# Gated attention outputs turned by transposing transfers, and one joining copy moved on ScalarE, in a two-layer encoder trunk

## Chip, cores and metric

The kernel runs on one core of a Trainium2 chip. The metric is the device time of one execution in microseconds (us), the median of several runs.

## The reference

The program is two layers of a hybrid encoder block over 256 tokens (two halves of 128, called `hf` 0 and 1 below) with a model width of 1024. Cut to the parts that matter here:

```
u = rms_norm(h, g_mix_pre)
(gq, gk, gv, gg, ra_f, ra_b, aq, ak, av, gate_a, gate_b) = split(u @ w_in)
o_gla    = rms_norm(o_f + o_b, g_gla_out)             # gated linear attention, both directions
branch_a = (o_gla * silu(gg)) @ w_o_gla               # 256x1024 @ 1024x1024
branch_b = gqa_attention(q, k, v) @ w_o_attn
mixed    = sigmoid(gate_a) * branch_a + sigmoid(gate_b) * branch_b
h = h + rms_norm(mixed @ w_out, g_mix_post)
gate, up = split(rms_norm(h, g_ffn_pre) @ w_ffn_in)   # 2 x 2816 columns
h = h + rms_norm((silu(gate) * up) @ w_ffn_out, g_ffn_post)
h = h + rms_norm(sigmoid(h @ w_ple_gate) * (p[i] @ w_ple_proj), g_ple_post)
```

The change concerns `o_gla * silu(gg)`, which has to stand feature by token before it can be the stationary operand of the product with `w_o_gla`, and `silu(gate) * up`, which has to be turned in the same way for `w_ffn_out`.

## The kernel before

All matrix products run on TensorE with each fp32 operand split into a high and a low fp32r part (`split`, L132: ScalarE casts the high part, VectorE subtracts it from the source for the low part), in three passes (`passes`, L122, and `mm`, L106). Weights are streamed from HBM in units of 128x2048 words (1 MB). `Stream` (L247) holds two raw buffers and four pairs `wh`/`wl`; a unit is one load on SP's queue, two 128x1024 casts on ScalarE and two 128x1024 subtractions on VectorE (all L134). A unit's raw buffer is loaded again once VectorE has subtracted from it. TensorE needs 24 matmuls of 128x512 for a plain unit (two token halves), and 12 for a unit inside a group of seven products that replace eight (`seven`, L713; weights in tiles `lent` and `big`, with 128x2048 additions on VectorE, L326 to L337).

Work that is not a weight product is written as `Task`s (L376): generators that are stepped by `tick` (L398), twice per twelve large matmuls or so, and that say after how many ticks they go on. So a number such as `W["g"]` or `WAIT_TURNED` sets where in the instruction order a step is put. Each engine executes its own instructions in that order; `tc.high_priority` and `tc.issue_after` move single ones.

Two ways of turning a block of 128 tokens x 512 features stand in the code:

- `transpose_in` (L445): four TensorE transposes against an identity matrix (L449) into a PSUM bank, then `split` from there.
- `turn_out` and `take_in` (L455, L472), used for the FFN's hidden values: ScalarE takes the 32-bit words apart into two planes of 16 bits (L468, or L463 where a block holds both token halves), SP issues one transposing transfer SBUF to SBUF (L469) of 128 x 1024 16-bit values, and `WAIT_TURNED` = 9 ticks later ScalarE joins the planes again (the "joining copy", L476), after which `split` works from SBUF.

The gate stage. `out_gate` (L1451) computes `sg = sigmoid(gg) * gg * o_gla` for each token half (L1457 on ScalarE, four 128x512 multiplications on VectorE, L127) and calls `turn_in` (L549), which waits 6 ticks and runs `transpose_in` on both 512-column blocks into `gT`. `GATES` = "uuu1u2m34m5m67m" (L1536) sets the order around it: u are the units of gate A, digits the seven products of gate B, m the four units of `gT @ w_o_gla`; `out_gate` must be done before the first m. TensorE's names there are `acc_0gate` (layer 0) and `acc_1gate`.

The FFN. The first two blocks of 256 hidden columns are computed by token half; after each half, the 512 values of both blocks (`first`) go to `turned` (L1573), which calls `turn_out` and, 9 ticks later, `take_in`. Each call takes a new 128x1024 tile `mid` for planes and result. The other blocks go the same way; only the last pair is turned by `transpose_in`.

SP's queue issues all weight loads and all transposing transfers in order: an entry that waits for its operand holds up those behind it.

Of the kernel before, what the change touches and what calls it, by code (L numbers as in the profile page):

```python
# [13 lines left out]
U16 = mybir.dt.uint16  # L14
# [4 lines left out]
P = 128  # L19
T = 256  # L20
# [9 lines left out]
WAIT_NEXT, WAIT_IN, WAIT_H = (7, 9), ((6, 9), (6, 6)), ((3, 5), (3, 5))  # L30
WAIT_MIX = 3, 6
WAIT_SPREAD = 12
W = dict(r=5, z=6, s0=4, s=3, s1=9, o0=1, o=1, k=4, q=3, a0=1, a1=4, a2=4, a3=1, g=6)

STEPS_FIRST = "00 10 01 11 02 12 03 13".split()
STEPS = "00 01 02 10 03 11 12 13".split()
# [24 lines left out]
def trunk_kernel(ctx: ExitStack, tc: tile.TileContext, a: dict, out: bass.AP):  # L61
# [7 lines left out]
    nc = tc.nc  # L69
# [11 lines left out]
    part = ["start"]  # L81
# [8 lines left out]
    def mid(dt=F32):  # L90
        return b4p.tile([P, 1024], dt, tag="mid", name=nm("mid"))
# [40 lines left out]
    def split(hi, lo, src):  # L132

        return nc.scalar.copy(hi, src), nc.vector.tensor_tensor(out=lo, in0=src, in1=hi.bitcast(F32), op=ALU.subtract)  # L134


    h = cp.tile([P, 2, D], F32, tag="h", name="h")
# [314 lines left out]
        if plain is not None:  # L452
            nc.scalar.copy(plain, ps[:, : n * P])

    def turn_out(src, k, hf):  # L455

        with tc.high_priority(AHEAD):
            both, turned = halves(mid())
            turned = turned.bitcast(U16)
            parts = both.bitcast(U16).rearrange("p (s c) -> p s c", s=2)  # L460
            words = src.bitcast(U16)
            if hf is None:
                nc.scalar.copy(  # L463
                    parts.rearrange("p s (k h f) -> p s k h f", k=2, f=P),
                    words.rearrange("p (h k f s) -> p s k h f", h=2, f=P, s=2),
                )
            else:
                nc.scalar.copy(parts, words.rearrange("p (c s) -> p s c", s=2))  # L468
            nc.sync.dma_start_transpose(out=turned.rearrange("p (x t) -> p x t", t=P), in_=parts.rearrange("p s c -> p (s c)"))  # L469
        return both, turned  # L470

    def take_in(sp, both, turned, k, hf):  # L472

        n, tn = (2, T) if hf is None else (4, P)
        hi, lo = sp.at(k, n, (hf or 0) * P, tn)
        nc.scalar.copy(  # L476
            both.bitcast(U16).rearrange("p (k t s) -> p k t s", s=2, t=tn),
            turned.rearrange("p (s k t) -> p k t s", s=2, t=tn),
        )
        split(hi, lo, both.rearrange("p (k t) -> p k t", t=tn))  # L480

    last_pow = [None]

# [62 lines left out]
    def halves(t):  # L546
        return [t[:, j * 512 : (j + 1) * 512] for j in range(2)]

    def turn_in(sp, x, hf, wait, plain=None, apart=False):  # L549


        def turn():
            yield wait
            for j, y in enumerate(halves(x)):
                if j and apart:
                    yield 1
                transpose_in(sp, y, 4 * j, 4, hf, plain and plain[j])

        sp.makers[hf].append(Task(turn(), part[0]))
# [489 lines left out]
    for l in range(DEPTH):  # L1049
# [31 lines left out]
        def put_ranks(o, hf):  # L1081
# [9 lines left out]
            with tc.high_priority(EMPTY):  # L1091
# [7 lines left out]
                nc.vector.tensor_copy(r[:, :, 64:80], r[:, :, 0:16])  # L1099
            yield W["r"]  # L1100
            ps = aux()
# [57 lines left out]
        o = {}  # L1159
# [20 lines left out]
        def keys(o):  # L1180
# [19 lines left out]
            for hf in range(2):  # L1200
                yield W["k"]
                ps = aux()
# [57 lines left out]
        def attend(g):  # L1260
            qs = []
            for hf in range(2):
                yield W["q"]
                ps = aux()
# [6 lines left out]
            keys.need()  # L1271
            yield W["a0"]
            prs = []
            for hf in range(2):
                prs.append(softmax(g, hf, qs[hf]))
                yield W["a1"]
            for hf in range(2):
# [21 lines left out]
        for x in range(2):  # L1299
            for i, o in enumerate(project_t(uT)):  # L1300
                dst, r = qk[:, x, i, :], 1.0 if x else P**-0.5
# [141 lines left out]
        gg = big().rearrange("p (s c) -> p s c", s=2)  # L1443
        for j in range(2):
            o = project(uT)
            for hf in range(2):
                dst = gg[:, hf, j * 512 : (j + 1) * 512]
                nc.scalar.activation(dst, o[hf], AF.Copy, bias=0.0, scale=rows[hf])
        gT = Split()

        def out_gate():  # L1451
            while not (gla.over and attention.over):
                yield 1
            for hf in range(2):
                sg = mid()
                with tc.issue_after(last_exp[0].ins):
                    nc.scalar.activation(sg, gg[:, hf, :], AF.Sigmoid)  # L1457
                for j, t in enumerate(halves(sg)):
                    s = slice(j * 512, (j + 1) * 512)
                    vmul(t, t, gg[:, hf, s])  # L1460
                    vmul(t, t, on[:, hf, s])
                turn_in(gT, sg, hf, W["g"])

        ogate = Task(out_gate(), f"{l}gg")

# [101 lines left out]


        part[0] = f"{l}ffnin"
        hid = Split()  # L1570
        us = [[ws.take() for _ in range(2)] for _ in range(2)]

        def turned(src, k, hf):  # L1573

            def turn():
                if k == 2 * PAIRS[-1]:
                    yield WAIT_LAST[hf]
                    transpose_in(hid, src, k, 4, hf)
                else:
                    x = turn_out(src, k, hf)  # L1580
                    yield WAIT_TURNED
                    take_in(hid, *x, k, hf)

            t = Task(turn(), part[0], k // 4)
            for i in range(2) if hf is None else (hf,):
                hid.makers[i].append(t)

        for hf in range(2):
            ws.lend = hf == 1
            first = t512()  # L1590
            for b in range(2):
                o = acc()
                for kh in range(2):
                    amode(o, u2, hf, kh * 4, us[b][kh], kh == 0, kh == 1, fresh=b == 0)
                sg = first[:, b * 256 : (b + 1) * 256]
# [35 lines left out]
        o = []  # L1631
# [21 lines left out]
        for x in FFN:  # L1653
# [3 lines left out]
            if x == "o":  # L1657
                n, w = outs.pop(0), ws.take()
# [117 lines left out]
```

## Time and profile before

| | us |
|---|---|
| median of 3 runs | 910.03 (909.97 to 911.33) |
| the profiled execution | 909.68 |
| its span (first to last instruction) | 907.9 |
| TensorE busy / VectorE busy / ScalarE busy | 898.8 / 790.2 / 620.5 |
| gate stage with merge, layer 0 / layer 1 (TensorE on `acc_gate`, then `acc_merge`) | 135.4 to 223.9 / 591.3 to 679.8 |

The profiled execution lies 0.35 us under the median, and 1.78 us of it are outside its span. In the rows of the profile, a start is given in us from the span's beginning, followed by the duration; `x4` is the count of like instructions merged into the row; a bracket such as `[0.55 <-DMA lent_0gate]` is the time for which the engine was idle before the row, and what ended that.

### The profile page before, as it was taken

The page shows a single profiled execution, that of the slowest core. Times are in us where ns is not written, and L with a number is a line of the kernel's source. Part 1 is how long each engine was busy: PE and PEld are TensorE (multiplying, and loading weights), DVE is VectorE, ACT ScalarE, POOL GpSimd, SP SyncE. Part 2 cuts the span into 40 slices and gives each one's busy share as a digit, 9 for nine tenths or more (in the row PEclk, how much of TensorE's full clock was granted, in tenths as well). Part 3 has the DMA queues.
Part 4 walks back from the last instruction along what each step waited for, and adds up shares of the span by engine and source line. Part 5 has one row for each costly group of instructions (what it writes and reads, how often), then busy time and mean ns, then how long its engine had stood idle before and what let it go on. Part 6 is the DMA issues. An engine that isn't in the chain of part 4 may idle for free.

```text
span 907.9 us, 12157 instructions
## 1 busy us (share of the span) xinstructions
PE 898.8 (99%) x4479; PEld 762.2 (84%) x4479; DVE 790.2 (87%) x1021; ACT 620.5 (68%) x1011; POOL 105.9 (12%) x157
## 2 busy tenths in 40 slices
PE   9999999999999999999999999999999999999997
PEld 8898888888888887887898888888888888888886
DVE  7999989987668999998779899799876799999984
ACT  7688677564467787756676687675644796958563
POOL 3700221300100000000254001110000000000001
PEclk9999999999999999999999999999999999999999
DMA  8663445657397594956576424455573966858461
GB/s 283 219 189 136 140 140 191 216 187 249 115 288 204 173 301 146 317 170 233 180 279 204 168 93 140 139 186 185 186 241 100 309 180 206 254 210 264 150 231 47
DMA packets 108519, 178.16 MB, mean 196 GB/s; under 512 B 22494, under 2 KB 46566, under 8 KB 107948
## 3 DMA queue, kind: packets, MB, share of 16 engines
q1 hardware_dynamic: 108300, 177.25, 59.9%
q8 instruction: 35, 0.57, 0.3%
q14 instruction: 24, 0.20, 0.1%
q10 hardware_dynamic: 160, 0.14, 0.0%
HBM read 169.50 MB, written 3.15 MB: 190 GB/s over the span
## 4 chain that ended last, share of the span: by engine, by line
PE 78%; DVE 11%; DMA 4%; issue 4%; ACT 2%; POOL 0%; SPq 0%; POOLq 0%; ACTq 0%; DVEq 0%
PE acc_1ffnin L122 12%; PE acc_0gate L122 7%; PE acc_1gate L122 7%; PE acc_1ffnin L106 7%; DVE wl_0ffnin L134 6%; PE acc_1rq L122 3%; PE acc_0gqk L106 2%; PE acc_1gqk L106 2%; PE acc_1wout L122 2%; PE acc_0ple L122 2%; PE acc_1v L122 2%; PE acc_0gg L122 2%; PE acc_1gg L122 2%; PE acc_0v L122 2%; PE acc_0merge L122 2%
## 5 line engine op out<-in xcount | busy, mean ns | idle before, releaser
L134 ACT CAST wh_0ffnin<-raw_0ffnin 128x1024 fp32r<-128x1024 f32 x38 | 38.1, 1048 | 19.8 <-DMA raw_0ffnin<-in_w_ffn_out_dram 10.2
L134 ACT CAST wh_1ffnin<-raw_1ffnin 128x1024 fp32r<-128x1024 f32 x38 | 38.3, 1048 | 17.4 <-DMA raw_1ffnin<-in_w_ffn_out_dram 5.0
L134 DVE TENSOR_TENSOR wl_0ffnin<-raw_0ffnin,wh_0ffnin 128x1024 fp32r<-128x1024 f32 x38 | 44.6, 1219 | 5.8 <-ACT wh_0ffnin L134 5.8
L134 DVE TENSOR_TENSOR wl_1ffnin<-raw_1ffnin,wh_1ffnin 128x1024 fp32r<-128x1024 f32 x38 | 44.8, 1219 | 5.0 <-ACT wh_1ffnin L134 4.9
L106 PE MATMUL acc_0ffnin<-wh_0ffnin,big_0ffnin 128*128 128x512 f32 x176 | 45.4, 392 | 0.0
L106 PE MATMUL acc_1ffnin<-wh_1ffnin,big_1ffnin 128*128 128x512 f32 x176 | 45.1, 390 | 0.0
L122 PE MATMUL acc_0ffnin<-wh_0ffnin,big_0wout 128*128 128x512 f32 x168 | 41.8, 390 | 0.0
L122 PE MATMUL acc_1ffnin<-wh_1ffnin,big_1wout 128*128 128x512 f32 x168 | 41.5, 389 | 0.0
L106 PEld LDWEIGHTS acc_0ffnin<-wh_0ffnin,big_0ffnin 128*128 128x128 f32 x176 | 32.8, 188 | 7.5 <-DVE big_0ffnin L134 0.5
L106 PEld LDWEIGHTS acc_1ffnin<-wh_1ffnin,big_1ffnin 128*128 128x128 f32 x176 | 33.0, 188 | 6.9
L122 PEld LDWEIGHTS acc_0ffnin<-wh_0ffnin,big_0wout 128*128 128x128 f32 x168 | 31.4, 188 | 7.1 <-ACT wh_0ffnin L134 0.4
L122 PEld LDWEIGHTS acc_1ffnin<-wh_1ffnin,big_1wout 128*128 128x128 f32 x168 | 31.5, 188 | 6.5
L134 DVE TENSOR_TENSOR wl_1ffnin<-lent_1ffnin,wh_1ffnin 128x1024 fp32r<-128x1024 f32 x30 | 35.7, 1217 | 0.6 <-ACT wh_1ffnin L134 0.6
L134 DVE TENSOR_TENSOR wl_0ffnin<-lent_0ffnin,wh_0ffnin 128x1024 fp32r<-128x1024 f32 x30 | 35.6, 1216 | 0.1
L134 ACT CAST wh_1ffnin<-lent_1ffnin 128x1024 fp32r<-128x1024 f32 x30 | 30.7, 1051 | 5.4 <-PE acc_1ffnin L106 3.9
L134 ACT CAST wh_0ffnin<-lent_0ffnin 128x1024 fp32r<-128x1024 f32 x30 | 30.4, 1053 | 3.6 <-DVE lent_0ffnin L332 3.4
L134 ACT CAST wh_0gate<-raw_0gate 128x1024 fp32r<-128x1024 f32 x20 | 19.9, 1049 | 14.4 <-DMA raw_0gate<-in_w_o_attn_dram 6.1
L134 ACT CAST wh_1gate<-raw_1gate 128x1024 fp32r<-128x1024 f32 x20 | 19.9, 1048 | 13.9 <-PE acc_1gate L122 5.9
L134 DVE TENSOR_TENSOR wl_0gate<-raw_0gate,wh_0gate 128x1024 fp32r<-128x1024 f32 x20 | 24.2, 1257 | 5.2 <-ACT wh_0gate L134 5.1
L134 DVE TENSOR_TENSOR wl_1gate<-raw_1gate,wh_1gate 128x1024 fp32r<-128x1024 f32 x20 | 23.5, 1221 | 5.1 <-ACT wh_1gate L134 5.1
L106 PE MATMUL acc_0ffnin<-wl_0ffnin,big_0ffnin 128*128 128x512 f32 x88 | 24.6, 394 | 0.6 <-DVE wl_0ffnin L134 0.6
L106 PE MATMUL acc_1ffnin<-wl_1ffnin,big_1ffnin 128*128 128x512 f32 x88 | 24.0, 391 | 0.0
(730 smaller groups left out, 2731.7 us busy)
## 6 DMA issues: line engine op xcount, KB each, us to landing
raw_0ffnin<-in_w_ffn_out_dram SPq DMA_DIRECT2D x11, 1024.0 KB, 5.9
raw_1ffnin<-in_w_ffn_out_dram SPq DMA_DIRECT2D x11, 1024.0 KB, 5.5
lent_0ffnin<-in_w_ffn_in_dram SPq DMA_DIRECT2D x6, 1024.0 KB
lent_1ffnin<-in_w_ffn_in_dram SPq DMA_DIRECT2D x6, 1024.0 KB, 7.5
raw_0v<-in_w_in_dram SPq DMA_DIRECT2D x4, 1024.0 KB, 5.8
raw_0gate<-in_w_o_gla_dram SPq DMA_DIRECT2D x4, 1024.0 KB, 6.8
raw_0gate<-in_w_o_attn_dram SPq DMA_DIRECT2D x4, 1024.0 KB, 5.2
raw_0wout<-in_w_ffn_in_dram SPq DMA_DIRECT2D x8, 512.0 KB, 4.6
```

Source lines behind the costliest of these rows:

```text
L106: return nc.tensor.matmul(o, lhsT, rhs, start=start, stop=stop)
L122: nc.tensor.matmul(o, x, y, start=start and n == 0, stop=stop and n == len(seq) - 1, **kw)
L134: return nc.scalar.copy(hi, src), nc.vector.tensor_tensor(out=lo, in0=src, in1=hi.bitcast(F32), op=ALU.subtract)
```

## The change

The gated attention outputs are no longer turned by TensorE: `out_gate` calls `turn_out` for each of the four blocks of 128 x 512 (two halves, two blocks each) as soon as the block is multiplied, and a task joins and splits them `WAIT_GATED` = 9 and 11 ticks later (the second block of a half one tick after the first). The planes are written over `gg`, and the turned values over `sg`. In the FFN, too, the turned values now go back into the source tile `t512`, and the planes of two successive blocks share one tile `mid`. The task of the first block of the first half (`(k, hf) == (0, 0)`) goes on only once the second half has been taken apart, and its joining copy is put behind that instruction on ScalarE.

```diff
--- before.py
+++ after.py
@@ -30,7 +30,8 @@
 WAIT_NEXT, WAIT_IN, WAIT_H = (7, 9), ((6, 9), (6, 6)), ((3, 5), (3, 5))
 WAIT_MIX = 3, 6
 WAIT_SPREAD = 12
-W = dict(r=5, z=6, s0=4, s=3, s1=9, o0=1, o=1, k=4, q=3, a0=1, a1=4, a2=4, a3=1, g=6)
+W = dict(r=5, z=6, s0=4, s=3, s1=9, o0=1, o=1, k=4, q=3, a0=1, a1=4, a2=4, a3=1)
+WAIT_GATED = 9, 11
 
 STEPS_FIRST = "00 10 01 11 02 12 03 13".split()
 STEPS = "00 01 02 10 03 11 12 13".split()
@@ -452,32 +453,29 @@
         if plain is not None:
             nc.scalar.copy(plain, ps[:, : n * P])
 
-    def turn_out(src, k, hf):
+    def turn_out(src, parts, mixed=False):
 
         with tc.high_priority(AHEAD):
-            both, turned = halves(mid())
-            turned = turned.bitcast(U16)
-            parts = both.bitcast(U16).rearrange("p (s c) -> p s c", s=2)
-            words = src.bitcast(U16)
-            if hf is None:
-                nc.scalar.copy(
-                    parts.rearrange("p s (k h f) -> p s k h f", k=2, f=P),
+            planes, words = (t.bitcast(U16) for t in (parts, src))
+            if mixed:
+                apart = nc.scalar.copy(
+                    planes.rearrange("p (s k h f) -> p s k h f", s=2, k=2, f=P),
                     words.rearrange("p (h k f s) -> p s k h f", h=2, f=P, s=2),
                 )
             else:
-                nc.scalar.copy(parts, words.rearrange("p (c s) -> p s c", s=2))
-            nc.sync.dma_start_transpose(out=turned.rearrange("p (x t) -> p x t", t=P), in_=parts.rearrange("p s c -> p (s c)"))
-        return both, turned
-
-    def take_in(sp, both, turned, k, hf):
-
-        n, tn = (2, T) if hf is None else (4, P)
-        hi, lo = sp.at(k, n, (hf or 0) * P, tn)
-        nc.scalar.copy(
-            both.bitcast(U16).rearrange("p (k t s) -> p k t s", s=2, t=tn),
-            turned.rearrange("p (s k t) -> p k t s", s=2, t=tn),
-        )
-        split(hi, lo, both.rearrange("p (k t) -> p k t", t=tn))
+                apart = nc.scalar.copy(planes.rearrange("p (s c) -> p s c", s=2), words.rearrange("p (c s) -> p s c", s=2))
+        nc.sync.dma_start_transpose(out=words.rearrange("p (x t) -> p x t", t=P), in_=planes)
+        return apart
+
+    def take_in(hi, lo, src, parts, behind=None):
+
+        tn = hi.shape[-1]
+        with tc.issue_after(behind.ins) if behind is not None else nullcontext():
+            nc.scalar.copy(
+                parts.bitcast(U16).rearrange("p (k t s) -> p k t s", s=2, t=tn),
+                src.bitcast(U16).rearrange("p (s k t) -> p k t s", s=2, t=tn),
+            )
+        split(hi, lo, parts.rearrange("p (k t) -> p k t", t=tn))
 
     last_pow = [None]
 
@@ -1459,7 +1457,16 @@
                     s = slice(j * 512, (j + 1) * 512)
                     vmul(t, t, gg[:, hf, s])
                     vmul(t, t, on[:, hf, s])
-                turn_in(gT, sg, hf, W["g"])
+                xs = [(t, gg[:, hf, j * 512 : (j + 1) * 512]) for j, t in enumerate(halves(sg))]
+                for x in xs:
+                    turn_out(*x)
+
+                def turn(hf=hf, xs=xs):
+                    for j, x in enumerate(xs):
+                        yield WAIT_GATED[hf] if j == 0 else 1
+                        take_in(*gT.at(4 * j, 4, hf * P, P), *x)
+
+                gT.makers[hf].append(Task(turn(), part[0]))
 
         ogate = Task(out_gate(), f"{l}gg")
 
@@ -1567,7 +1574,7 @@
 
 
         part[0] = f"{l}ffnin"
-        hid = Split()
+        hid, spare, apart = Split(), [], {}
         us = [[ws.take() for _ in range(2)] for _ in range(2)]
 
         def turned(src, k, hf):
@@ -1577,9 +1584,15 @@
                     yield WAIT_LAST[hf]
                     transpose_in(hid, src, k, 4, hf)
                 else:
-                    x = turn_out(src, k, hf)
+                    if not spare:
+                        spare.extend(halves(mid()))
+                    parts = spare.pop()
+                    apart[k, hf] = turn_out(src, parts, hf is None)
                     yield WAIT_TURNED
-                    take_in(hid, *x, k, hf)
+                    while (k, hf) == (0, 0) and (0, 1) not in apart:
+                        yield 1
+                    dst = hid.at(k, 2, 0, T) if hf is None else hid.at(k, 4, hf * P, P)
+                    take_in(*dst, src, parts, apart[0, 1] if (k, hf) == (0, 0) else None)
 
             t = Task(turn(), part[0], k // 4)
             for i in range(2) if hf is None else (hf,):
```

What this does to the order of instructions, at three places. The first is ScalarE in layer 0's gate stage, from the last cast of the operand sums (`mid_0gate<-t_0gate`) on: `wh_0gate` are weight casts, `aux_0gg` the PSUM banks with the turned outputs, `big_0gg` the tiles of `gT`. Before:

```order
L134 CAST mid_0gate_1693<-t_0gate_1626 128x512
L134 CAST wh_0gate_1680<-lent_0gate_1670 128x1024 x2
L134 CAST wh_0gate_1747<-raw_0gate_1676 128x1024 x2
L134 CAST big_0gg_1719<-aux_0gg_1714 128x4x128
L134 CAST big_0gg_1727<-aux_0gg_1722 128x4x128
L134 CAST big_0gg_1719<-aux_0gg_1730 128x4x128
L134 CAST big_0gg_1727<-aux_0gg_1737 128x4x128
L1475 ACTIVATE big_0gate_1744<-acc_0gate_1598,rs_start_120 128x512
L1475 ACTIVATE big_0gate_1744<-acc_0gate_1599,rs_start_121 128x512
L134 CAST wh_0gate_1781<-big_0gate_1672 128x1024 x2
L134 CAST wh_0gate_1805<-raw_0gate_1678 128x1024
```

After the change, the same place (`big_0gg_1276` is `gg`, now also holding the planes; L466 takes apart, L474 joins):

```order
L466 COPY big_0gg_1276<-mid_0gg_1636 128x1024 x2
L135 CAST wh_0gate_1688<-lent_0gate_1678 128x1024
L466 COPY big_0gg_1276<-mid_0gg_1646 128x1024 x2
L135 CAST wh_0gate_1688<-lent_0gate_1678 128x1024
L1482 ACTIVATE big_0gate_1722<-acc_0gate_1598,rs_start_120 128x512
L1482 ACTIVATE big_0gate_1722<-acc_0gate_1599,rs_start_121 128x512
L135 CAST wh_0gate_1725<-raw_0gate_1684 128x1024 x2
L474 COPY big_0gg_1276<-mid_0gg_1636 128x1024 x2
L135 CAST big_0gg_1753<-big_0gg_1276 128x4x128
L135 CAST big_0gg_1763<-big_0gg_1276 128x4x128
L135 CAST wh_0gate_1767<-big_0gate_1680 128x1024 x2
L474 COPY big_0gg_1276<-mid_0gg_1646 128x1024 x2
```

Eight copies have come in among the weight casts. Behind the last row stand two more casts into `gT`, the copy of the first product out of PSUM, and then the casts of `raw_0gate_1686`, the weights of the first m, which in the old order are those of `raw_0gate_1678` in the last row. TensorE's sixteen transposes of that place, and the sixteen of layer 1, are gone from its order. The second place is SP's queue there. Before:

```order
L297 DMA lent_0gate_1670<-in_w_in_dram 128x4x512
L297 DMA lent_0gate_1674<-in_w_in_dram 128x4x512
L297 DMA raw_0gate_1678<-in_w_o_gla_dram 128x4x512
L372 DMA ggla_1gla_4924<-in_g_gla_out_dram 128x256
L297 DMA raw_0gate_1753<-in_w_o_gla_dram 128x4x512
```

After the change:

```order
L298 DMA lent_0gate_1678<-in_w_in_dram 128x4x512
L298 DMA lent_0gate_1682<-in_w_in_dram 128x4x512
L467 DMA_TRANSPOSE mid_0gg_1636<-big_0gg_1276 128x8x128 x2
L467 DMA_TRANSPOSE mid_0gg_1646<-big_0gg_1276 128x8x128 x2
L298 DMA raw_0gate_1686<-in_w_o_gla_dram 128x4x512
L373 DMA ggla_1gla_4912<-in_g_gla_out_dram 128x256
L298 DMA raw_0gate_1731<-in_w_o_gla_dram 128x4x512
```

The load of the first m's weights (`raw_0gate_1678`, now `raw_0gate_1686`) stands behind four transposing transfers. The third place is ScalarE at the start of layer 0's FFN, from the first half's taking apart on (`t_0ffnin` are the hidden values, L1596 the Silu). Before:

```order
L468 COPY mid_0ffnin_2665<-t_0ffnin_2594 128x1024
L476 COPY mid_0ffnin_2665<-mid_0ffnin_2665 128x1024
L1596 ACTIVATE t_0ffnin_2668<-acc_0ffnin_2669 128x256
L134 CAST wh_0ffnin_2702<-raw_0wout_2522 128x1024 x2
L134 CAST mid_0ffnin_2729<-mid_0wout_2297 128x512
L134 CAST mid_0ffnin_2738<-mid_0wout_2298 128x512
L134 CAST mid_0ffnin_2747<-mid_0wout_2298 128x512
L134 CAST wh_0ffnin_2755<-raw_0emb_2589 128x1024 x2
L1596 ACTIVATE t_0ffnin_2668<-acc_0ffnin_2711 128x256
L134 CAST wh_0ffnin_2764<-lent_0ffnin_2696 128x1024 x2
L468 COPY mid_0ffnin_2752<-t_0ffnin_2668 128x1024
```

After the change:

```order
L466 COPY mid_0ffnin_2657<-t_0ffnin_2586 128x1024
L1609 ACTIVATE t_0ffnin_2660<-acc_0ffnin_2661 128x256
L135 CAST wh_0ffnin_2694<-raw_0wout_2514 128x1024 x2
L135 CAST mid_0ffnin_2721<-mid_0wout_2289 128x512
L135 CAST mid_0ffnin_2730<-mid_0wout_2290 128x512
L135 CAST mid_0ffnin_2739<-mid_0wout_2290 128x512
L135 CAST wh_0ffnin_2746<-raw_0emb_2581 128x1024 x2
L1609 ACTIVATE t_0ffnin_2660<-acc_0ffnin_2703 128x256
L135 CAST wh_0ffnin_2755<-lent_0ffnin_2688 128x1024 x2
L466 COPY mid_0ffnin_2657<-t_0ffnin_2660 128x1024
L474 COPY mid_0ffnin_2657<-t_0ffnin_2586 128x1024
```

The joining copy has moved from the second row to the last one. Layer 1's FFN had its first joining copy behind the second taking apart already. In both layers some later joining copies come one or two weight casts later than before.

## The prediction

> **What bounds the kernel.** I read the page's busy shares first, then the waits of TensorE (PE), then the chain of work that ended last.
>
> ```profile
> PE 898.8 (99%) x4479; PEld 762.2 (84%) x4479; DVE 790.2 (87%) x1021; ACT 620.5 (68%) x1011; POOL 105.9 (12%) x157
> PE 78%; DVE 11%; DMA 4%; issue 4%; ACT 2%; POOL 0%; SPq 0%; POOLq 0%; ACTq 0%; DVEq 0%
> ```
>
> PE is busy for 898.8 of 907.9 us and makes up 78% of the chain. What it waits for is listed by the view of waits (engine, line, releaser: us, times, longest):
>
> ```profile
> PE acc_0ffnin L106 <- DVE wl_0ffnin L134: 0.6, 2, 0.3
> PE acc_0ffnin L122 <- DVE wl_0ffnin L134: 0.2, 1, 0.2
> PE aux_0ffnout L449 <- DVE h L611: 0.2, 1, 0.2
> ```
>
> Those are all of its waits behind the start, all of them in layer 0's FFN. So PE's work is the time, except there. The chain (start, duration, work) has the transposes that go:
>
> ```profile
> 147.86 1.75 PE aux_0gg L449 x16
> 149.60 51.71 PE acc_0gate L122 x228
> 603.70 1.75 PE aux_1gg L449 x16
> 268.26 5.66 DMA mid_0ffnin<-mid_0ffnin
> ```
>
> Both sets of sixteen transposes lie on the chain, with matmuls right behind; and at 268.26 the chain of layer 0's FFN starts with a transposing transfer, not with a matmul.
>
> **The change part by part. TensorE's transposes.** Sixteen of them hold the chain for 1.75 us in either layer, so removing them takes 2 x 1.75 = 3.5 us, if PE then finds its operands ready. The Trainium skill, page "TensorE: Matmul & The Clock Gate", Part 4, gives about 275 ns for one transpose in a kernel; sixteen would be 4.4 us a layer and the saving 8.8 us. The chain decides: transposes overlap, and sixteen take 1.75 us, not 4.4.
>
> **What comes in their place.** The FFN shows each new operation with the same shape (count, ns min/median/max; then us to landing):
>
> ```profile
> L468 ACT COPY mid_0ffnin<-t_0ffnin x6: 1038/1044/1047, 267.2 to 376.0; 128x1024 uint16<-128x1024 uint16 x6
> L476 ACT COPY mid_0ffnin<-mid_0ffnin x9: 1168/1177/1183, 274.0 to 380.8; 128x1024 uint16<-128x1024 uint16 x9
> L469 SPq DMA_TRANSPOSE mid_0ffnin<-mid_0ffnin x9: 1237/1250/1922, 268.3 to 377.1; - x9
> DMA to landing us min/median/max: 3.3/3.6/4.3
> ```
>
> Per layer: four taking apart at 1.05 us and four joining at 1.18 us, 8.9 us more on ScalarE (ACT); four transfers of 1.24 us each on SP's queue, landing 3.3 to 4.3 us after issue. The casts and subtractions into `gT` stay, four each, from SBUF instead of PSUM: I cost that at nothing, since the FFN's like rows differ by under 0.05 us. ACT's idle time in layer 0's gate stage is the cover (start, duration, work, idle before):
>
> ```profile
> 143.46 2.00 ACT L134 CAST wh_0gate<-lent_0gate 128x1024 fp32r<-128x1024 f32 x2 [0.55 <-DMA lent_0gate<-in_w_in_dram]
> 146.98 2.00 ACT L134 CAST wh_0gate<-raw_0gate 128x1024 fp32r<-128x1024 f32 x2 [1.51 <-PE acc_0gate L122]
> 148.89 2.04 ACT L134 CAST big_0gg<-aux_0gg 128x512 fp32r<-128x512 f32 x4
> 150.80 1.29 ACT L1475 ACTIVATE big_0gate<-acc_0gate,rs_start 128x512 f32<-128x512 f32 x2
> 154.20 2.01 ACT L134 CAST wh_0gate<-big_0gate 128x1024 fp32r<-128x1024 f32 x2 [2.11 <-PE acc_0gate L122]
> 156.92 1.06 ACT L134 CAST wh_0gate<-raw_0gate 128x1024 fp32r<-128x1024 f32 x1 [0.71 <-PE acc_0gate L122]
> 160.55 0.69 ACT L1475 ACTIVATE big_0gate<-acc_0gate,rs_start 128x512 f32<-128x512 f32 x1 [1.14 <-PE acc_0gate L122]
> 162.41 1.06 ACT L134 CAST wh_0gate<-lent_0gate 128x1024 fp32r<-128x1024 f32 x1 [1.17 <-PE acc_0gate L122]
> 170.52 2.01 ACT L134 CAST wh_0gate<-raw_0gate 128x1024 fp32r<-128x1024 f32 x2 [2.91 <-PE acc_0gate L122]
> ```
>
> Idle: 0.55 + 1.51 + 2.11 + 0.71 + 1.14 + 1.17 + 2.91 = 10.1 us, nearly all of it waiting for PE; so 8.9 us fit by 172, but on the way ACT runs late. I walk it in the new order, against the point where PE first needs what is late. The VectorE (DVE) and PE rows for that:
>
> ```profile
> 143.70 1.28 DVE L127 TENSOR_TENSOR mid_0gg<-mid_0gg,big_0gla 128x512 f32<-128x512 f32 x2
> 146.11 1.28 DVE L127 TENSOR_TENSOR mid_0gg<-mid_0gg,big_0gla 128x512 f32<-128x512 f32 x2
> 165.60 3.49 DVE L134 TENSOR_TENSOR wl_0gate<-lent_0gate,wh_0gate 128x1024 fp32r<-128x1024 f32 x3
> 165.79 1.98 PE L122 MATMUL acc_0gate<-wh_0gate,big_0gg 128*128 128x512 f32 x8
> raw_0gate<-in_w_o_gla_dram SPq DMA_DIRECT2D x4, 1024.0 KB, 6.8
> ```
>
> DVE finishes the first block of half 0 halfway through the row at 143.70, so the first two takings apart run 144.4 to 146.5; one weight cast to 147.5; the second two, ready at 147.4, to 149.6; a cast to 150.6; two sigmoids (1.29) to 151.9; two casts to 153.9; two joins to 156.3; two 512-column casts (half of 2.04) to 157.3; two casts to 159.3; two joins to 161.6; two casts into `gT` to 162.7; the copy of the first product (at most a sigmoid's 0.65) to 163.3; then the weights of the first m, 164.3 and 165.3. PE starts that m at 165.79 - 1.75 = 164.04, needs the second half of `wh` 0.9 us later, and `wl` 1.8 and 2.3 us later (four, eight and ten matmuls; the chain's 228 in 51.71 us give 0.227 each). That is 0.3 us late with full durations. In the rows, neighbours overlap (two casts in 2.00, each 1.05 alone), which over some twenty instructions gives about 1.1 us: then it is early by 0.9. DVE follows ACT by 1.2 us a piece (3.49 for three): 165.5 and 166.6 against 165.85 and 166.3. Price: 0 to 0.3 us a layer; I take 0, as overlap is what the rows show. `gT` itself is ready at 163 to 164, its second half needed only at 166.8.
>
> The joins wait for transfers: issued 145.5 to 149.6, landing 3.3 to 4.3 us later, 153.9 at the latest; the second joins start at 159.3. The load behind them on SP's queue (`raw_0gate_1686`) goes at 149.6 + 1.24 = 150.9, lands 6.8 us later at 157.7 and is cast from 163.3 on: 5.6 us to spare. Layer 1's chain repeats layer 0's 455.84 us later (603.70 against 147.86), so the walk holds twice.
>
> The Trainium skill speaks against the swap: "VectorE: DVE Perf Modes", section "The three transpose paths", has 390 ns on TensorE and 1309 ns by DMA for a 128x128 bf16 block, and its rules prefer TensorE where PSUM will do. An estimate by that page: 10.5 us for a transfer of eight such blocks, 41.9 for four, the weights behind them at 195 instead of 164, and a time near 967. The trace has 3.3 to 4.3 us for eight blocks, so that price does not hold here; the mechanism is weighed as the third rival.
>
> **Layer 0's FFN.** SP, ACT, DVE and PE there, in that order:
>
> ```profile
> 283.93 1.25 SPq L469 DMA_TRANSPOSE mid_0ffnin<-mid_0ffnin  x1
> 274.00 1.17 ACT L476 COPY mid_0ffnin<-mid_0ffnin 128x1024 uint16<-128x1024 uint16 x1 [5.76 <-DMA mid_0ffnin<-mid_0ffnin]
> 290.24 1.18 ACT L476 COPY mid_0ffnin<-mid_0ffnin 128x1024 uint16<-128x1024 uint16 x1 [3.38 <-DMA mid_0ffnin<-mid_0ffnin]
> 275.48 0.43 DVE L127 TENSOR_TENSOR t_0ffnin<-acc_0ffnin,t_0ffnin 128x256 f32<-128x256 f32 x1 [6.25 <-ACT t_0ffnin L1596]
> 293.92 2.35 DVE L134 TENSOR_TENSOR wl_0ffnin<-raw_0ffnin,wh_0ffnin 128x1024 fp32r<-128x1024 f32 x2
> 277.00 1.98 PE L122 MATMUL acc_0ffnin<-wh_0ffnin,big_0wout 128*128 128x512 f32 x8
> 293.33 2.30 PE L122 MATMUL acc_0ffnin<-wh_0ffnin,big_0wout 128*128 128x512 f32 x8
> 295.46 0.62 PE L122 MATMUL acc_0ffnin<-wl_0ffnin,big_0wout 128*128 128x512 f32 x2
> 296.33 0.74 PE L122 MATMUL acc_0ffnin<-wl_0ffnin,big_0wout 128*128 128x512 f32 x2 [0.24 <-DVE wl_0ffnin L134]
> 341.39 0.63 PE L106 MATMUL acc_0ffnin<-wl_0ffnin,big_0ffnin 128*128 128x512 f32 x2
> 342.36 0.73 PE L106 MATMUL acc_0ffnin<-wl_0ffnin,big_0ffnin 128*128 128x512 f32 x2 [0.35 <-DVE wl_0ffnin L134]
> 419.61 0.62 PE L106 MATMUL acc_0ffnin<-wl_0ffnin,big_0ffnin 128*128 128x512 f32 x2
> 420.48 0.73 PE L106 MATMUL acc_0ffnin<-wl_0ffnin,big_0ffnin 128*128 128x512 f32 x2 [0.25 <-DVE wl_0ffnin L134]
> ```
>
> The joining copy stands at the head of ACT's queue for 5.76 us, and DVE behind it idles for 6.25. Then DVE runs to 300 without a gap, and PE waits for it at 296: eight matmuls take 2.13 us instead of 1.81, two take 0.87 instead of 0.45: 0.74 us lost. In the same way two take 0.97 at 341 (0.52 lost) and 0.87 at 419 (0.42). Sum 1.68 us. With the copy moved, the next Silu waits only for PE's bank. Half 1's second block ends at 277.0, its first one 24 matmuls or 5.4 us earlier, less 1.75: the Silu is at 269.9 instead of 275.2, behind the join. What is late next is the second Silu, whose bank is done at 275.3; ACT's four casts and three short ones between them last 5.5 us, to 275.7, so that wait costs nothing, and ACT and DVE are 5 us ahead of before. The second join idled for 3.38 us until 290.24, its transfer having landed 6.3 us after 283.93; now the transfer goes at about 279 and lands by 285.3 at the same pace. So the subtraction of 293.92 comes at about 290, while PE wants it 1.75 earlier: DVE gains some 2 us on PE, the 0.74 goes, and with it what the chain carries on (DVE and transfers only, from 268 to 425): 0.94. Bounds: nothing below, if loads hold the pace, and 2.6 us at most (the quoted 1.68 and about 0.9 in slower matmuls beside those rows). I take 1.7, the quoted rows. Reusing `t512` and `mid` costs nothing: each tile's next writer stands behind the join on ACT anyway.
>
> Sum against the profiled execution: 909.68 - 3.5 - 1.7 = 904.5. The median is 0.35 higher, so **904.8 us**.
>
> **Rivals.** *Only the transposes' time comes back.* If loads, not ACT, set layer 0's FFN, its stalls stay: 910.03 - 3.5 = 906.5. For it: the chain there passes through weight loads, too; against it, the 6.25 us of idle DVE.
>
> *ACT gives the gain back in the gate stage.* Every us by which the first m's weights come later than the walk's 164.3 is a us of PE in either layer. If 1.75 us more is lost there (the overlaps of 0.9 us lost, and joins that take 0.2 us more than the 1.18 beside weight casts, would do it), the transposes' gain is gone and the FFN's 1.7 is left: 908.3. For it: 8.9 us go into 10.1 us of idle time. Against it: neighbouring copies overlap in every row quoted.
>
> *Transfers one after the other: slower than before.* The trace shows no four of them in a row. If each begins when the last has landed (3.6 us, the median), the fourth lands at 145.5 + 4 x 3.6 = 159.9; the load behind it lands at 166.7, and its first half is cast by 167.7, 3.7 us after PE wants it. Two layers: 910.03 - 5.2 + 2 x 3.7 = 912.2. It decides from 3.35 us each on (a stall of 2.6 us a layer against 5.2 gained). Against it: the queue issues one every 1.24 us, and its bytes (0.25 MB) are a quarter of a load that lands in 5 to 7 us.
>
> **Chances.** Forecast 0.55; only the transposes 0.18; given back 0.12; in a row 0.08; other losses, which leave about the old time, 0.07. The range goes from the FFN's upper bound (910.03 - 3.5 - 2.6 = 903.9, and 0.5 for the spread of runs: 903.4) to the third case's 908.3. Faster by over 0.2% (1.8 us, what a measurement here can tell from no change) holds for the first two and half of the third: 0.79; within, for the other half and most of the other losses: 0.11; slower, for the rest: 0.10.
>
> **What would show it.** Right: no L449 rows on `aux_0gg` and `aux_1gg`; the chain's gate matmuls of layer 0 ending at about 199.6 instead of 149.60 + 51.71 = 201.3; no PE wait on `wl_0ffnin` at 294 to 296; ACT's joins of `gg` without idle time before them. Wrong: a PE wait on `wh_0gate` or `wl_0gate` near 164 or 620; ACT idle before the joins until a DMA; PE's three FFN stalls still there.

## The result and the profile after

Over 22 runs the changed kernel takes 909.47 us (median; 903.69 to 912.67), the kernel before 910.34 us. The ratio is 0.9989 with a 95% interval of 0.9977 to 1.0001: no difference that the measurement can tell. Forecast were 904.8 us, with a range from 903.4 to 908.3. The profiled execution has a span of 907.2 us (907.9 before).

The page of the changed kernel (busy time by engine; the chain by engine):

```profile
PE 896.5 (99%) x4447; PEld 758.1 (84%) x4447; DVE 791.2 (87%) x1021; ACT 635.3 (70%) x1027; POOL 103.6 (11%) x157
PE 71%; DVE 14%; DMA 7%; issue 3%; ACT 3%; POOL 0%; POOLq 0%; SPq 0%; ACTq 0%; DVEq 0%
```

TensorE (PE) has 32 instructions fewer and is busy 2.3 us less, but its share of the chain fell from 78% to 71%, and DVE, the transfers and ACT got what it lost. The view of waits for PE says where (engine, line, releaser: us, times, longest):

```profile
PE acc_0ffnin L107 <- DVE wl_0ffnin L135: 1.4, 5, 0.4
PE acc_1ffnin L107 <- DVE wl_1ffnin L135: 0.6, 2, 0.4
PE acc_0ffnin L107 <- DVE big_0ffnin L135: 0.5, 1, 0.5
PE acc_0gate L123 <- ACT wh_0gate L135: 0.3, 1, 0.3
PE aux_0merge L450 <- DVE big_0gate L1527: 0.2, 1, 0.2
```

Layer 0's FFN still has waits, more of them than before, and layer 1's FFN has some, which had none. Yet the transposes are gone, ACT no longer idles for the first join, and the wait near 295 is gone, as rows of the changed kernel show (chain; ACT; ACT; PE):

```profile
594.02 61.20 PE acc_1gate L123 x270
153.32 2.25 ACT L474 COPY big_0gg<-mid_0gg 128x1024 uint16<-128x1024 uint16 x2
270.95 2.00 ACT L135 CAST wh_0ffnin<-raw_0wout 128x1024 fp32r<-128x1024 f32 x2
294.95 1.98 PE L123 MATMUL acc_0ffnin<-wh_0ffnin,big_0wout 128*128 128x512 f32 x8
```

The chain's gate matmuls of layer 1 are one piece of 270, with no transposes between 42 and 228. The joins of `gg` start at 153.32 without idle time ahead of them. At 270.95 ACT casts weights where before it idled for a transfer until 274.00, and PE passes 295 with eight matmuls in 1.98 us and no wait. So PE gained where it was to gain, and gave it back elsewhere. (Whether the last row is the moved copy's doing is taken up below.) To find the place, the same matmul is looked up in the timelines of two kernels. Each row has its start before and by how much another kernel's start differs; the last two columns are kernels of the experiments below. Each column is one execution: 908.97, 903.88 and 908.91 us, against medians of 909.47, 905.27 and 907.93. The times of the changed kernel spread over 9.0 us, those of the kernel before over 4.4, so the columns say where time goes, and the medians and ratios how much.

| Matmul (start before, us) | changed | all transfers raised | all raised but the last pair's |
|---|---|---|---|
| gate stage of layer 0, early (138.62) | +0.15 | +0.34 | +0.20 |
| behind the transposes' old place (149.36) | -1.52 | -1.33 | -1.47 |
| first of merge, layer 0 (201.15) | -0.95 | -1.44 | -0.92 |
| FFN, layer 0 (296.33) | -1.83 | -2.45 | -1.36 |
| FFN, layer 0 (342.36) | -2.16 | -3.15 | -1.96 |
| FFN, layer 0 (402.34) | -0.46 | -3.29 | -0.75 |
| first transpose of `h` behind it (426.41) | +0.01 | -4.63 | -1.57 |
| gate stage of layer 1, ahead of the transposes (594.70) | -0.16 | -4.91 | -1.73 |
| behind their old place (605.21) | -1.83 | -6.58 | -3.40 |
| FFN, layer 1 (842.98) | -1.84 | -6.15 | -2.12 |
| FFN, layer 1 (852.27) | -0.69 | -6.10 | -0.89 |
| first transpose of `h` behind it (873.39) | -0.65 | -6.02 | -0.89 |

The changed kernel is 2.16 us ahead at 342 and level at 426: layer 0's FFN took 2.2 us back in its second half. Layer 1's gate stage gave 1.67 us again, and 1.15 us of that went between 843 and 852. At 374 us stands what happened. SP's queue before and after (start, duration, work):

```profile
374.00 4.44 SPq L469 DMA_TRANSPOSE mid_0ffnin<-mid_0ffnin  x2
378.54 0.53 SPq L297 DMA_DIRECT2D raw_0ffnin<-in_w_ffn_in_dram  x1
```

```profile
371.52 1.24 SPq L467 DMA_TRANSPOSE t_0ffnin<-mid_0ffnin  x1
372.87 0.57 SPq L298 DMA_DIRECT2D raw_0ffnin<-in_w_ffn_in_dram  x1
374.96 2.21 SPq L467 DMA_TRANSPOSE t_0ffnin<-mid_0ffnin  x1
```

Before, the two transposing transfers of the last pair of blocks that goes this way were issued one after the other (at 374.00 and 377.10; the row's 4.44 us span both), and the 1 MB weight load behind them. Now the load stands between them. ACT's joining copies (L476 before, L474 now) there, before and after, and after also the taking apart for the second transfer (L466; in brackets the idle time before a row and what ended it):

```profile
379.75 2.26 ACT L476 COPY mid_0ffnin<-mid_0ffnin 128x1024 uint16<-128x1024 uint16 x2 [0.76 <-DMA mid_0ffnin<-mid_0ffnin]
```

```profile
373.89 1.05 ACT L466 COPY mid_0ffnin<-t_0ffnin 128x1024 uint16<-128x1024 uint16 x1 [0.16 <-DVE t_0ffnin L128]
377.96 1.18 ACT L474 COPY mid_0ffnin<-t_0ffnin 128x1024 uint16<-128x1024 uint16 x1 [1.12 <-DMA t_0ffnin<-mid_0ffnin]
382.47 1.17 ACT L474 COPY mid_0ffnin<-t_0ffnin 128x1024 uint16<-128x1024 uint16 x1 [2.67 <-DMA t_0ffnin<-mid_0ffnin]
```

The issue of the second transfer began as soon as it could (its operand is ready at 373.89 + 1.05 = 374.94, the issue begins at 374.96), but the load was in the queue ahead of it. It lands late, and ACT stands idle for 2.67 us with weight casts queued behind the join. DVE and PE then, and the transfer as the chain has it (from the start of its issue to its landing), all of the changed kernel:

```profile
384.62 2.36 DVE L135 TENSOR_TENSOR wl_0ffnin<-raw_0ffnin,wh_0ffnin 128x1024 fp32r<-128x1024 f32 x2 [2.23 <-ACT wh_0ffnin L135]
```

```profile
387.04 0.74 PE L107 MATMUL acc_0ffnin<-wl_0ffnin,big_0ffnin 128*128 128x512 f32 x2 [0.25 <-DVE wl_0ffnin L135]
400.74 0.73 PE L107 MATMUL acc_0ffnin<-wl_0ffnin,big_0ffnin 128*128 128x512 f32 x2 [0.26 <-DVE wl_0ffnin L135]
401.87 0.73 PE L107 MATMUL acc_0ffnin<-wl_0ffnin,big_0ffnin 128*128 128x512 f32 x2 [0.40 <-DVE wl_0ffnin L135]
```

```profile
374.96 7.49 DMA t_0ffnin<-mid_0ffnin
823.55 6.41 DMA t_1ffnin<-mid_1ffnin
```

DVE idles 2.23 us, where it had been busy without a gap. PE is short of `wl` for the first time 2.4 us later and again at 400.74 and 401.87; from 386 to 402 its lead shrinks by 1.70 us. The chain holds the same transfer in layer 1, at 823.55. The diff has the cause in plain sight: `dma_start_transpose` stood inside `with tc.high_priority(AHEAD):` and now stands one level further out, behind the block. Only the taking apart is still raised; the issue now stands behind loads that come earlier in the program. Against the kernel with all transfers raised, shown below, three transfers in each layer's FFN have one load more ahead of them: the second of the last pair, and two earlier ones (in layer 0 those issued at 312.50 and 329.92). In layer 0 the load of a gain has moved, too (`mid_0ffnout`, from 390.05 before the change to 404.55), in among the loads of the output weights.

### The profile page after: what moved, and what is told of

It reads as the page before. It is cut to its first block, busy times and chain, and to the rows that moved or that the text cites. A ratio compares the mean times of both kernels' runs of the same rounds, so it can differ in the third digit from the quotient of the medians.

```text
span 907.2 us, 12121 instructions
## 1 busy us (share of the span) xinstructions
PE 896.5 (99%) x4447; PEld 758.1 (84%) x4447; DVE 791.2 (87%) x1021; ACT 635.3 (70%) x1027; POOL 103.6 (11%) x157
## 3 DMA queue, kind: packets, MB, share of 16 engines
HBM read 169.50 MB, written 3.15 MB: 190 GB/s over the span
## 4 chain that ended last, share of the span: by engine, by line
PE 71%; DVE 14%; DMA 7%; issue 3%; ACT 3%; POOL 0%; POOLq 0%; SPq 0%; ACTq 0%; DVEq 0%
PE acc_1ffnin L123 10%; PE acc_1gate L123 7%; PE acc_0ffnin L123 5%; DVE wl_0ffnin L135 5%; PE acc_1ffnin L107 5%; DVE wl_0gate L135 3%; PE acc_1rq L123 3%; PE acc_0gqk L107 2%; PE acc_1gqk L107 2%; PE acc_1wout L123 2%; PE acc_0ple L123 2%; PE acc_1gg L123 2%; PE acc_1v L123 2%; PE acc_0v L123 2%; PE acc_1merge L123 2%
```

## The experiments

Each kernel was timed in five rounds. The first four ran together on one chip (the kernel before: 910.06 us), the last four on another (909.41 us), so kernels of the two sets are compared by their ratios to the kernel before. The kernel with all transfers raised has 5 runs, the others 8 to 12.

| Kernel | Median, us | Ratio to before, 95% interval |
|---|---|---|
| all transfers raised | 905.27 | 0.9940, 0.9926 to 0.9955 |
| before, transfers not raised | 911.95 | 1.0026, 1.0011 to 1.0040 |
| gate part alone | 906.29 | 0.9958, 0.9945 to 0.9971 |
| FFN part alone, raised | 909.60 | 0.9991, 0.9982 to 1.0000 |
| last pair alone raised | 905.71 | 0.9962, 0.9947 to 0.9977 |
| all raised but the last pair | 907.93 | 0.9979, 0.9963 to 0.9995 |
| all raised, first join back | 906.12 | 0.9965, 0.9954 to 0.9977 |
| gate part alone, not raised | 910.20 | 1.0002, 0.9990 to 1.0013 |

**All transfers raised.** The changed kernel with one line indented:

```diff
-        nc.sync.dma_start_transpose(out=words.rearrange("p (x t) -> p x t", t=P), in_=planes)
+            nc.sync.dma_start_transpose(out=words.rearrange("p (x t) -> p x t", t=P), in_=planes)
```

> The changed kernel with its transposing transfers issued inside the block of raised priority again, as in the kernel before; nothing else. Theory Q (queue order): the changed kernel lost its gain because the transfers of the FFN's pairs went into SP's queue behind a weight load (layer 0: issued at 374.96 after a load at 372.87, where before both went at 374.00 together; 2.2 us of TensorE lost from 387 to 426; layer 1: 823.55 after a load at 822.14, 1.1 us lost). Then this kernel is 3.3 us faster than the changed one, 4.2 us faster than the kernel before: ratio about 0.9954, and TensorE does not fall back against the kernel before between 387 and 426 and at 849. Rival L (loads): layer 0's FFN is held by DVE and weight loads, which take back whatever TensorE gained earlier, in whatever order the queue stands: ratio about 0.999, the same loss at the same place.

Measured: 905.27 us, ratio 0.9940. Theory Q holds (its 0.9954 lies just inside the interval); rival L's 0.999 lies outside. Four spaces turn a change worth nothing into one worth 4.8 us by the medians (5.5 by the ratio). In its profile the two transfers go ahead of the load and the joins run back to back again (SP's queue; ACT):

```profile
370.10 4.69 SPq L467 DMA_TRANSPOSE t_0ffnin<-mid_0ffnin  x2
374.84 0.57 SPq L298 DMA_DIRECT2D raw_0ffnin<-in_w_ffn_in_dram  x1
```

```profile
375.79 2.25 ACT L474 COPY mid_0ffnin<-t_0ffnin 128x1024 uint16<-128x1024 uint16 x2 [0.33 <-DMA t_0ffnin<-mid_0ffnin]
```

PE's waits in this kernel are these two, neither in an FFN, and the chain of layer 0's FFN is PE's from 261.82 on:

```profile
PE warm L107 <- POOL seed L144: 1.0, 1, 1.0
PE aux_1wout L450 <- DVE mid_1wout L542: 0.2, 1, 0.2
```

```profile
261.82 65.31 PE acc_0ffnin L123 x288
327.13 5.44 PE acc_0ffnin L107 x24
332.57 5.44 PE acc_0ffnin L123 x24
```

In the changed kernel, the chain leaves PE in the middle of that stretch:

```profile
262.44 35.41 PE acc_0ffnin L123 x156
298.26 3.42 DVE wl_0ffnin L135 x3
302.11 5.11 DMA raw_0ffnin<-in_w_ffn_in_dram
```

**Before, transfers not raised.** The opposite edit in the kernel before: its line 469 is moved out of the block.

```diff
-            nc.sync.dma_start_transpose(out=turned.rearrange("p (x t) -> p x t", t=P), in_=parts.rearrange("p s c -> p (s c)"))
+        nc.sync.dma_start_transpose(out=turned.rearrange("p (x t) -> p x t", t=P), in_=parts.rearrange("p s c -> p (s c)"))
```

> The kernel before with one edit: its transposing transfers are issued outside the block of raised priority, as in the changed kernel. Theory Q: 2.2 + 1.1 = 3.3 us slower, ratio about 1.0036, with the same late second transfer of the last pair in both layers. Rival L: the order of the queue costs nothing that loads would not cost anyway, ratio 1.000.

Measured: 1.0026, slower by 2.4 us (1.0 to 3.6). The moved issue costs time without any other part of the change. The expected 1.0036 lies inside the interval, rival L's 1.000 outside. The loss shows in the same place: PE falls back by 1.34 us between 386 and 402, and by 0.36 between 843 and 852.

**Gate part alone.** The kernel before, with the diff's part in `out_gate` and copies of the new `turn_out` and `take_in` that only it calls:

```diff
-                turn_in(gT, sg, hf, W["g"])
+                xs = [(t, gg[:, hf, j * 512 : (j + 1) * 512]) for j, t in enumerate(halves(sg))]
+                for x in xs:
+                    gate_out(*x)
...
+                gT.makers[hf].append(Task(turn(), part[0]))
```

> The kernel before with the gated outputs turned by transfers as in the changed kernel, the FFN as before (its transfers inside the block of raised priority, the first joining copy where it was). Theory Q: 1.66 us per layer for sixteen transposes, less 0.9 us that layer 0's gate and merge stages take back by late loads (183 and 228 us in the changed kernel's trace): about 2.4 us faster, ratio 0.9974. Rival L: layer 0's part is taken back in its FFN, only layer 1's 1.7 us is left: ratio 0.9982; with layer 1 taken back as well 1.000.

Measured: 0.9958, a gain of 3.8 us by the medians (2.6 to 5.0 by the interval). The expected 2.4 us was too low and rival L is out in both forms. Part of the surplus lies in layer 0's FFN, where PE gains 1.35 us between 402.34 and 426.41 although the FFN is as before; nothing here says why. The gated transfers of this kernel are as little raised as in the changed one, but on SP's queue all four still stand together ahead of the next load.

**FFN part alone, raised.** The kernel with all transfers raised, and this in `out_gate` in place of the transfers:

```diff
+                turn_in(gT, sg, hf, 6)
```

> The changed kernel with the gated outputs turned on TensorE as before, and the FFN's transfers inside the block of raised priority: only the reuse of tiles and the moved first joining copy are left of the change. Theory Q: the three stalls of layer 0's FFN go (1.5 us, of which 1.39 were seen to go in the changed kernel's trace between 264 and 342), ratio 0.9983. Rival L: they go at 296 and come back as waits on loads before 426: ratio 1.000.

Measured: 0.9991, 0.8 us faster, with an interval (0.9982 to 1.0000) that holds theory Q's 0.9983 just so and rival L's 1.000 at its other end. By itself this is inconclusive. In its trace PE is 1.40 us better off at 426.41 than ahead of the gate stage (from +0.28 to -1.12), and 0.91 of that are lost again by 594.70, in stages that the change doesn't touch. Two short waits in layer 0's FFN are left (0.2 us each).

**Last pair alone raised.** The changed kernel, with

```diff
+        with tc.high_priority(AHEAD) if raised else nullcontext():
+            nc.sync.dma_start_transpose(out=words.rearrange("p (x t) -> p x t", t=P), in_=planes)
...
+                    apart[k, hf] = turn_out(src, parts, hf is None, k == 2 * PAIRS[-2] and hf is not None)
```

> The changed kernel with raised priority for the issue of the last pair's two transfers alone (in each layer those at 371 to 375 and 820 to 824 us): they go together ahead of the load again, the five other transfers of the pairs and blocks stand behind loads as in the changed kernel. Theory P (the last pair's second transfer behind the load carries the loss): about 1 us slower than the kernel with all transfers raised (905.27), so about 906.3, ratio 0.995 to 0.996. Rival E (the earlier transfers, at 312 and 327 us, carry it): about 3 us slower than that, near the changed kernel, ratio 0.998 to 0.999.

**All raised but the last pair.** The same, with the condition turned round:

```diff
+                    apart[k, hf] = turn_out(src, parts, hf is None, k != 2 * PAIRS[-2])
```

> The complement: all transfers of the FFN issued with raised priority but the last pair's two. Theory P: about 3 us slower than the kernel with all raised, 908.3, ratio 0.998; ScalarE idles for over 2 us ahead of a joining copy near 380 and 827, and the load of a gain stands between output weights near 404. Rival E: about 1 us slower, ratio 0.995 to 0.996.

Measured: 0.9962 with the last pair raised, 0.9979 with all but it. Theory P said 0.995 to 0.996 and 0.998, rival E 0.998 to 0.999 and 0.995 to 0.996; neither interval holds what E said of it. The last pair carries the larger part. The rows that theory P named for the second kernel are there: ACT idles 3.10 us ahead of the join at 829.80, the load of the gain stands at 404.25, and in layer 0 (ACT, idle time ahead of the last pair's second join):

```profile
382.17 1.18 ACT L475 COPY mid_0ffnin<-t_0ffnin 128x1024 uint16<-128x1024 uint16 x1 [3.51 <-DMA t_0ffnin<-mid_0ffnin]
```

Its column in the table above loses 1.21 us between 342 and 402 and 1.23 between 843 and 852, where the kernel with all raised gains 0.14 and loses 0.05. The load of the gain moves back and forth with the last pair, so in layer 0 no run separates the two; layer 1 has no such load, and loses its 1.23 us all the same.

**All raised, first join back.** From the kernel with all transfers raised, the other half of the FFN's edit is taken out:

```diff
-                    while (k, hf) == (0, 0) and (0, 1) not in apart:
-                        yield 1
...
-                    take_in(*dst, src, parts, apart[0, 1] if (k, hf) == (0, 0) else None)
+                    take_in(*dst, src, parts)
```

> The kernel with all transfers raised, but with the first joining copy where it was before, ahead of the taking apart of the second half (the reuse of tiles and the gated transfers stay). If the moved copy is what ended the stalls of layer 0's FFN: 1.4 us slower than with it, ratio about 0.9955, and ScalarE idle for over 5 us near 268. If it is worth nothing once the transposes are gone from the gate stage (the FFN-only kernel gained 0.9 us at most with certainty): ratio 0.994 to 0.9945.

Measured: 0.9965 (0.9954 to 0.9977): 2.3 us slower than 0.9940 by the ratios, and 0.994 to 0.9945 lies outside its interval. So the moved join is probably worth something; the expected 0.9955 (1.4 us) is inside, but the intervals of the two kernels just touch (0.9954 and 0.9955). ACT idles again, for somewhat less than the 5 us named, and a stall of PE is back (ACT; PE):

```profile
270.53 1.17 ACT L474 COPY mid_0ffnin<-t_0ffnin 128x1024 uint16<-128x1024 uint16 x1 [4.76 <-DMA t_0ffnin<-mid_0ffnin]
```

```profile
339.50 0.73 PE L107 MATMUL acc_0ffnin<-wl_0ffnin,big_0ffnin 128*128 128x512 f32 x2 [0.40 <-DVE wl_0ffnin L135]
```

Two pair transfers of layer 0, near 325 and 330, also change places with a load each in this kernel, so the 2.3 us are not the join's alone for certain.

**Gate part alone, not raised.** The kernel of the gate part alone, with line 469's issue moved out of its block as in the second experiment.

> The kernel before with gated transfers, and all transfers outside the block of raised priority; tiles and first joining copy as before. It asks whether late transfers cost more once the transposes are gone. If their price is that measured in the kernel before (2.4 us): 906.29 + 2.4 = 908.7, ratio 0.9984. If TensorE, being earlier by 3 us, has less slack on them (4.2 us, the difference of the changed kernel and its raised form): 910.5, ratio 1.0004.

Measured: 1.0002 (0.9990 to 1.0013). The 3.8 us of the gate part are gone, with the FFN's tiles and joins as before; PE falls back by 1.53 us between 386 and 402. The second expectation's 1.0004 lies inside the interval and the first one's 0.9984 outside, which speaks for late transfers costing more here than in the kernel before.

## Why the prediction was wrong

**The step that failed** is the price of nothing for the rewritten `turn_out` in the FFN. The sentence for it is that reusing `t512` and `mid` costs nothing, since each tile's next writer stands behind the join on ACT. No run shows a cost of the reuse itself (the kernel with the first join back has it, at 0.9965, and the gate part alone has not, at 0.9958; their intervals overlap). But the rewriting also took the transfer's issue out of the block of raised priority, and the sum has no term for that. Loads came ahead of three transfers in each layer, which together cost 4.2 us by the medians. SP's queue was compared in the gate stage, where the transfers are new, and not in the FFN, where they were old. None of the rivals named this; about the old time had 0.07, as "other losses".

Two signs were in sight. The section on the change says that in both layers some later joining copies come one or two weight casts later; with all transfers raised, those of layer 1 and of layer 0's last pair stand on ACT where they stood before. And the prediction's own rows show that a transfer behind loads can be late: those issued at 268.26 and 283.93, with weight loads ahead of them, ended ACT's idle time at 274.00 and 290.24, 5.7 and 6.3 us after their issue began, not 3.3 to 4.3.

The sum otherwise, step by step:

- **The transposes' 3.5 us: right.** The starts move by 1.67 us in both layers (from +0.15 to -1.52 and from -0.16 to -1.83), and the gate part alone gained 3.8 us. PE's wait at 183 to 184 takes some of it back in layer 0 in some executions: 0.57 us to the merge stage in the changed kernel, none with all transfers raised, though the order of the queue is the same there. So the gate matmuls end at 200.2 in the changed kernel and not at the 199.6 named as a sign.
- **ACT's walk through the gate stage: right.** The joins started without idle time, and no wait appears on `wh_0gate` or `wl_0gate` near 164 or 620. The casts of the first m's weights began at 162.09; the walk has them from 163.3, or 162.2 with its 1.1 us of overlap. The four transfers in a row, the rival for slower, did not run one after the other: they went out in 6.1 us, as the second row has it, and in layer 1 the fourth landed 7.4 us after the first was issued (601.19 to 608.55), not 4 x 3.6 = 14.4 us (ACT; SP's queue).

```profile
162.09 2.00 ACT L135 CAST wh_0gate<-raw_0gate 128x1024 fp32r<-128x1024 f32 x2
145.66 6.09 SPq L467 DMA_TRANSPOSE mid_0gg<-big_0gg  x4
```

- **The FFN's 1.7 us: right on ACT, not shown on PE.** ACT ran as forecast: the second transfer goes at 279.58 (forecast about 279) and is joined at 285.27 (285.3). But of the three stalls of PE that make up the 1.7 us, only one follows the moved copy. The table has what PE gains at each, against the kernel before:

| Stall of the kernel before | forecast, us | all raised | FFN part alone | first join back | gate part alone |
|---|---|---|---|---|---|
| 293.33 to 296.33 | 0.74 | 0.74 | 0.74 | 0.73 | 0.43 |
| 341.39 to 342.36 | 0.52 | 0.52 | 0.52 | -0.16 | -0.16 |
| 419.61 to 420.48 | 0.42 | 0.41 | 0.01 | 0.41 | 0.41 |

The first stall goes in the last two kernels, too, where the copy stands as before (and in every other kernel here), so the missing wait at 294 to 296, named as a sign, tells nothing of the copy. The third goes with the gate part and not with the FFN part. Why these two go is open. In the changed kernel itself the three gains are 0.73, 0.15 and -0.01. By the times, the FFN part is worth 0.8 us alone, and between the kernels with and without it 1.0 by the medians (905.27 against 906.29) or 1.6 by the ratios (0.9940 against 0.9958, with overlapping intervals).
- **The sum.** With the issue left where it was, the forecast of 904.8 (5.2 us less) meets 905.27 (4.8 less; 5.5 by the ratio). That is partly luck: by the medians the gate part gave 3.8 for its 3.5 and the FFN part 1.0 for its 1.7, and not by the stalls named. What the sum left out is worth 4.2 us by the medians, 4.5 by the ratios.

**Why so much for one transfer.** Layer 0's FFN has DVE and PE nearly level: the chain goes mostly through DVE and transfers from 298 on in the changed kernel and through PE in the raised one. From 384.62 to 408 DVE has no idle time in which to make up its 2.23 us, so a delay of ACT becomes one of PE. In the kernel before the same move costs 2.4 us, in the kernel with the gate part 4.0 (0.9958 to 1.0002). That PE, earlier by the transposes, has less slack fits this and was said ahead of the run; the two intervals overlap, so the size of the difference is not settled. Nor is the share of the earlier transfers: the ratios leave them 2.0 us (0.9962 against 0.9940), while PE's starts in the kernel with the last pair alone raised show no loss in either FFN against the one with all raised.

Why the transfer is late: its issue began at 374.96, 2.1 us behind the load's, and it landed at 382.45, 7.49 us later. With all transfers raised, the same one is issued at 373.56, ahead of the load, and ACT begins its join at 376.87, 3.3 us later. The Trainium skill, page "DMA: Bandwidth & Descriptors", section "Queues, rings and completion order", says that all that SP issues goes into one row of rings, and that each DMA engine takes what is in a ring in order. The rows here agree: 7.49 us with the load ahead, 3.3 without. But a load ahead does not always cost as much. The kernel before has the landing of four transfers in its profile; they took 3.3 to 4.3 us from the start of their issue, and two of them were issued 1.2 and 1.7 us behind a load. Nor does a late landing have to cost PE time: the changed kernel's transfer at 312.50 took 6.30 us and the one at 778.13 took 6.58, and PE's lead stays within 0.11 us there.

## What to carry to other kernels

When code that issues a transfer is rewritten, compare the whole queue that it stands in, old entries included, not only the entries that the change adds: an indentation took nine transfers of each layer out of a raised priority and cost nearly as much as the change gained. If a change with a sound gain measures as nothing, line up the same instruction in both traces; the stretch in which its lead shrinks is where to look for the cause. A sign proves a part of a change only if it stays away where that part is left out: the wait near 295 went in every kernel, with the moved copy and without. And a transfer that somebody waits for goes ahead of a load that nobody needs yet, on the same queue.

## What was not expected of the hardware

A transposing transfer of 128 x 1024 16-bit words behind a 1 MB load landed 7.49 us after its issue began in layer 0 and 6.41 us in layer 1, against 3.3 to 4.3 for the four of the kernel before whose landing its profile has. The issue itself took 2.21 us in layer 0 and the usual 1.24 in layer 1, so most of the delay comes after the issue. Four such transfers in a row went out in 6.1 us and held up neither ACT's joins nor the cast of the weights behind them: the serialising that the third rival feared does not show.
